# A hybrid transformer block on one core: the first local-attention query projection moved into the state-space core

## The chip, the cores and the metric

The kernel runs on one core of a Trainium2 chip, in one launch. The metric is the device time of that core in microseconds (us), as the median of the runs; lower is better. The engines are TensorE (PE), VectorE (DVE), ScalarE (ACT), GpSimd (POOL) and SyncE (SP, which issues most DMAs). Each engine works through its instructions in a fixed order; an instruction whose input isn't there makes those behind it on its engine wait as well.

## The reference

Two layers (DEPTH = 2) act on 256 latent tokens and, in layer 0, 256 context tokens, with a model width of 1024, all in float32. In each layer a normalized input is projected into three token mixers and three gates:

```python
(xbc_l, dt_l, k_l, v_l, ckv_l, kr_l, z_l, q_l, cq_l, gates_l) = split_cols(h_l @ w_in[i], IN_WIDTHS)
...
y_ssm_l, y_ssm_c = ssd_branch(...)      # Mamba-2 scan in both directions, 16 heads, gated by silu(z), RMS norm
y_swa_l, y_swa_c = swa_branch(...)      # local attention, 8 query heads of 128, 2 key/value heads
y_mla_l, y_mla_c = mla_branch(...)      # latent attention, 8 heads
x_l = x_l + gt1[:, None] * merge_branches(gates_l, y_ssm_l, y_swa_l, y_mla_l, ...)
x_l = x_l + gt2[:, None] * swiglu(modulate(x_l, norm2_g[i], sh2, sc2), w_ffn_in[i], w_ffn_out[i])
```

The change concerns the queries of the local attention. They are projected, normalized per head, and those of latent tokens rotated:

```python
ql = apply_axial_rope(rms_norm(q.reshape(bsz, n, 8, 128), q_g), *rope)
```

In layer 1 only the latent tokens are carried on.

## The kernel before, in words

**Precision.** Float32 products are made of three `fp32r` matmuls each: both operands are split into a high and a low part, and `mm3` (L146 to L148) adds hi*hi, hi*lo and lo*hi. A weight block of 128x1024 comes in by DMA (`raw`), ACT makes its high part (`hi`, L132) and DVE its low part (`lo`, L134). Token tiles have 128 rows: four in layer 0 (two latent, two context), two in layer 1.

**The order of the work.** The program is written as Python generators. `weave(main, fill)` (L57) runs a main generator and after each of its steps takes pieces of a fill generator, until the cost that these yield has used up the step's budget. `braid` (L71) and `chain` join fills, `drain` runs a rest to its end. What is written first has priority; a scheduler then puts each engine's instructions into an order by these priorities and by its own estimate of when the inputs will be there. The accumulators in PSUM come from three pools: `mm` (four buffers), `s` and `t` (two each); transposes and the core's `L930` share `t`.

**The stretch around the change** (`layer`, L1366):

- `ssm_core` (L823) is the main generator: (group, token tile, half) steps, 16 + 4 in layer 0 and 8 + 4 in layer 1, each with a budget F_SSM of 6.5 and 8.44. A step builds decay matrices on ACT, POOL and DVE (L889 `cb`, L910 `eb`, L911 `ef`), then PE multiplies them (`L922`, eight small matmuls, tile `s`) and adds the carried state (`L930`, tile `t`). `L932` scales the latter and `L934` adds the former (DVE, `yo`), `L940` (POOL) sums into `xs`, `L946` (DVE) multiplies by the gate `z`, and `L948` (ACT) sums its square.
- The fill is the gate projection `zproj`, then keys and values `swa_kv` braided with the first gates. Its yields add up to less than the core's budgets.
- Behind the core stands `ssm_out` (L977): the sums of squares (L982, L983), the reciprocal root on POOL (`ssr`, L160), the scaling of z (`L989`), and per 128 columns a transposition (`L995`) and the split into `yt` (L156, L157).
- Between the steps of `ssm_out` the code takes steps of `swa_q` (L1045), once per group g of four heads: q[0], then q[1]. A `swa_q` multiplies four weight blocks (96 matmuls of 128x512 in layer 0, 48 in layer 1, tiles `mm`), copies the result (ACT L1052 `qraw`), squares it (ACT L1054), sums per head (DVE `L1055`, `L1060`), takes the reciprocal root (POOL L160 `rsq`), multiplies it in (POOL `L1066`), rotates the latent tiles (`rope`: DVE `L555`, four `L561`, `L563`, tile `ro`), and transposes four heads (PE `L1076`, tile `t`), each followed by a split into high and low parts (`qT`).
- Then `attend` weaves the scores (mm3 into `s`, mask by `L1104`), the softmax (ACT L631) and the transposes of the probabilities (`L596`) with the remaining projections.

Of the kernel before, what the change touches and what calls it, by code (L numbers as in the profile page):

```python
# [70 lines left out]
def braid(n, a, b):  # L71

    for _ in range(n):
        yield next(a)
    for x in a:
        yield x
        y = next(b, None)
        if y is not None:
            yield y
    yield from b  # L80


def drain(gen):
    for _ in gen:
        pass


class Kern:
# [913 lines left out]
    def swa_kv(self, l, h):  # L1002
# [26 lines left out]
            w3 = lambda t: t[:, o].rearrange("p (h w) -> p h w", h=2)  # L1029
            self.rope(w3(ro), w3(kr[0]), p["rs"][1], tt, 2, P, w3(tmp))  # L1030
        yield 0.1
        self.kT, self.qT = [], {}
        for g in range(2):
            ps = self.PS("t")
            for tt in range(4):
# [256 lines left out]
    def gates(self, l, b, h, cols, out):  # L1292
        nc = self.nc
        n = cols.stop - cols.start
        for m in range(KT):
            ps = self.lin_a(self.d["w_g"][l, b * 8 + m], h, cols)
            if n == 512:
                t = self.U(name="gate")
                nc.scalar.activation(t, ps, AF.Tanh, scale=0.5)
                o = self.dr.tile([P, 512], F32, tag=f"gate{b}{m}", name=self.nm("gated"))  # L1300
                nc.scalar.dma_start(o, t)
                out.append(o)
            else:
                if m % 2 == 0:
                    u = self.U(name="gate")
                t = u[:, (m % 2) * 256 : (m % 2) * 256 + 256]
                nc.scalar.activation(t, ps, AF.Tanh, scale=0.5)
                out.append(t)
            yield n / 100
# [56 lines left out]
    def layer(self, l, x, h, norm):  # L1366
# [4 lines left out]
        tts = range(2) if last else range(4)  # L1371
        streams = (0,) if last else (0, 1)
        gt, merged = [[], [], []], [None] * KT
        gates = lambda b: self.gates(l, b, h, cols, gt[b])
# [2 lines left out]
        post = chain(self.ssm_inproj(l, h, norm), () if l else self.tables(l))  # L1377
        for _ in range(5):
            next(post)
        fill = chain(self.zproj(l, h, tts), braid(4, self.swa_kv(l, h), gates(0)))  # L1380
        drain(self.ssm_conv(l, h, last, post, fill))
        drain(post)
        if l == 0:
# [2 lines left out]
        drain(fill)  # L1386
        rows = iter(()) if last else self.mod_rows()
        next(rows, None)
        q = [self.swa_q(l, h, g, tts) for g in range(2)]

        out = self.ssm_out(tts)
        for _ in range(NQ):
            next(out, None)
            next(q[0])
        for _ in range(5):
            next(out, None)
            next(q[0], None)
            next(q[1])
        drain(out)
        drain(q[0])  # L1400
        ys = self.yssm
        self.pair, self.cqT = {}, None
        mod = iter(())
# [82 lines left out]
        h = []  # L1486
# [191 lines left out]
```

## Time and profile before

| | |
|---|---|
| median of 3 runs | 1853.46 us (1852.89 to 1855.38) |
| profiled execution: its own time | 1853.35 us |
| profiled execution: span of the core | 1851.5 us |
| mean granted TensorE clock | 0.999 |
| PE, DVE, ACT, POOL busy | 97%, 76%, 49%, 16% |
| chain that ended last | PE 67%, DVE 9%, issue 4%, ACT 4%, POOL 2% |

The time is that of the whole launch, the span runs from the first to the last instruction in the trace. Busy shares are means over the span. A row of a timeline gives an instruction's start, its duration, engine, source line, operation and tiles; a bracket at its end gives how long its engine had been idle before it and whose work ended that. Durations of consecutive matmuls overlap, so a matmul's price is read from start to start.

### The profile page before, as it was taken

Reading aid. Unit: us, or ns where it says so; the run is one execution under the profiler, and the core shown is the slowest. Engines: PE = TensorE matmul, PEld = TensorE weight load, DVE = VectorE, ACT = ScalarE, POOL = GpSimd, SP = SyncE. Lnnn points to the kernel's source line nnn. Section 1 sums busy time; section 2 is a strip of 40 time slices with the busy share of each in tenths; the row PEclk is TensorE's granted clock in tenths of the full one; section 3 lists DMA queues with packets and bytes.
Section 4 is the critical chain, followed back from the end, with each engine's and each line's share of the span. In section 5 each row is a group of like instructions: output and inputs, shape, how many; then the busy total and the mean of one; then the engine's idle time right before and its main releaser. Section 6 shows DMA issues by size and latency. Waiting matters only on the chain.

```text
span 1851.5 us, 28424 instructions
## 1 busy us (share of the span) xinstructions
PE 1797.0 (97%) x10180; PEld 1534.7 (83%) x10180; DVE 1411.7 (76%) x3090; ACT 916.3 (49%) x2025; POOL 294.0 (16%) x265
## 2 busy tenths in 40 slices
PE   8999999999999999999999999999999999999999
PEld 2886777778888888898888888887779988899999
DVE  3896876897799885569888875798788688786654
ACT  2557674444545653333323222547745677455442
POOL 3005433200013331100000000002421022210000
PEclk9999999999999999999999999999999999999999
DMA  8234353454443233536556553335334332255565
GB/s 301 91 106 149 113 176 99 136 199 158 136 166 105 99 120 113 189 109 198 193 184 203 183 188 117 105 103 182 117 123 135 107 106 85 90 181 171 183 181 139
DMA packets 102750, 270.22 MB, mean 146 GB/s; under 512 B 12897, under 2 KB 15761, under 8 KB 102609
## 3 DMA queue, kind: packets, MB, share of 16 engines
q1 hardware_dynamic: 93888, 254.06, 42.3%
q10 hardware_dynamic: 7056, 9.85, 1.5%
q0 software_dynamic: 1664, 4.50, 0.6%
q8 instruction: 80, 1.31, 0.3%
q14 instruction: 62, 0.50, 0.1%
HBM read 256.70 MB, written 11.67 MB: 145 GB/s over the span
## 4 chain that ended last, share of the span: by engine, by line
PE 67%; DVE 9%; issue 4%; ACT 4%; POOL 2%; DMA 1%; SPq 0%; POOLq 0%; ACTq 0%; DVEq 0%
PE mm L146 20%; PE mm L147 20%; PE mm L148 20%; DVE lo L134 3%; ACT hi L132 2%; PE t L596 1%; DVE junk L253 1%; PE s L146 1%; PE s L148 1%; PE s L147 1%; DMA eb<-scr 1%; DVE ptl L154 1%; DMA mraw<-in_w_modT 1%; DVE rmax L623 0%; POOL ef L896 0%
## 5 line engine op out<-in xcount | busy, mean ns | idle before, releaser
L132 ACT ACTIVATE hi<-raw 128x1024 fp32r<-128x1024 f32 (+1 forms) x350 | 356.7, 1021 | 582.1 <-PE mm L147 290.2
L134 DVE TENSOR_TENSOR lo<-raw,hi 128x1024 fp32r<-128x1024 f32 (+3 forms) x346 | 425.2, 1231 | 195.6 <-ACT hi L132 194.0
L146 PE MATMUL mm<-hh,hi 128*128 128x512 f32 (+1 forms) x1280 | 438.5, 345 | 4.1 <-ACT sq L676 1.9
L148 PE MATMUL mm<-hh,lo 128*128 128x512 f32 (+1 forms) x1280 | 435.8, 341 | 0.9 <-DVE lo L134 0.9
L147 PE MATMUL mm<-hl,hi 128*128 128x512 f32 (+1 forms) x1280 | 436.0, 341 | 0.6 <-DVE hl L346 0.5
L146 PEld LDWEIGHTS mm<-hh,hi 128*128 128x128 f32 x1280 | 241.7, 190 | 32.4 <-ACT sq L676 2.2
L148 PEld LDWEIGHTS mm<-hh,lo 128*128 128x128 f32 x1280 | 242.5, 190 | 28.7 <-DVE lo L134 1.3
L147 PEld LDWEIGHTS mm<-hl,hi 128*128 128x128 f32 x1280 | 242.5, 190 | 28.0 <-DVE hl L346 1.2
L146 PE MATMUL mm<-hi,hh 128*128 128x512 f32 (+2 forms) x368 | 142.5, 387 | 3.3 <-ACT hh L312 2.0
L147 PE MATMUL mm<-lo,hh 128*128 128x512 f32 (+2 forms) x368 | 138.9, 378 | 0.0
L148 PE MATMUL mm<-hi,hl 128*128 128x512 f32 (+2 forms) x368 | 136.9, 381 | 2.0 <-DVE hl L346 2.0
L253 DVE CUSTOM_DVE_ANT_0 junk<-mraw,crow,mod 128x512 bf16<-128x512 f32 x160 | 120.3, 752 | 3.5 <-DMA mraw<-in_w_modT 1.2
L253 DVE CUSTOM_DVE_ANT_0 junk<-mraw,crow 128x512 bf16<-128x512 f32 x160 | 110.3, 690 | 13.1 <-DMA mraw<-in_w_modT 11.8
L631 ACT ACTIVATE prob<-s,nm 128x512 f32<-128x512 f32 (+1 forms) x96 | 59.1, 615 | 56.3 <-DVE nm L628 30.4
L153 ACT ACTIVATE pth<-t 128x256 fp32r<-128x256 f32 x160 | 60.5, 388 | 46.9 <-DVE ptl L154 38.6
L146 PEld LDWEIGHTS mm<-hi,hh 128*128 128x128 f32 x368 | 69.8, 190 | 16.7 <-ACT hh L312 2.5
L148 PEld LDWEIGHTS mm<-hi,hl 128*128 128x128 f32 x368 | 69.1, 190 | 14.4 <-DVE hl L346 2.5
L147 PEld LDWEIGHTS mm<-lo,hh 128*128 128x128 f32 x368 | 69.6, 189 | 11.9 <-issue 2.9
L160 POOL TENSOR_TENSOR nrs<-nv,mhalf 128x2 f32<-128x2 f32 x7 | 5.2, 743 | 436.8 <-DVE nv L294 436.8
L146 PE MATMUL mm<-acth,hi 128*128 128x512 f32 (+1 forms) x198 | 72.7, 367 | 0.6 <-DVE xl L1352 0.6
L148 PE MATMUL mm<-acth,lo 128*128 128x512 f32 (+1 forms) x198 | 72.3, 365 | 0.0
L147 PE MATMUL mm<-actl,hi 128*128 128x512 f32 (+1 forms) x198 | 72.3, 365 | 0.0
(429 smaller groups left out, 4063.1 us busy)
## 6 DMA issues: line engine op xcount, KB each, us to landing
raw<-in_w_fi SPq DMA_DIRECT2D x88, 512.0 KB, 3.4
mraw<-in_w_modT SPq DMA_DIRECT2D x160, 256.0 KB, 4.6
raw<-in_w_g SPq DMA_DIRECT2D x48, 512.0 KB, 3.4
raw<-in_w_p SPq DMA_DIRECT2D x48, 512.0 KB, 3.3
raw<-in_w_fo SPq DMA_DIRECT2D x32, 512.0 KB, 3.6
raw<-in_w_xbc SPq DMA_DIRECT2D x24, 512.0 KB, 3.6
wm<-in_w_mod SPq DMA_DIRECT2D x32, 256.0 KB, 5.6
raw<-in_w_z SPq DMA_DIRECT2D x16, 512.0 KB, 3.2
```

The source lines that it names most:

```text
L132: nc.scalar.activation(hi[:, :n], raw[:, :n], AF.Copy)
L134: eng.tensor_tensor(lo[:, :n], raw[:, :n], hi[:, :n].bitcast(F32), ALU.subtract)
L146: mm(out, a[0], b[0], start=start, stop=False)
L147: mm(out, a[0], b[1], start=False, stop=False)
L148: mm(out, a[1], b[0], start=False, stop=stop)
L153: nc.scalar.activation(hi, src, AF.Copy)
L154: nc.vector.tensor_tensor(lo, src, hi.bitcast(F32), ALU.subtract)
L160: self.nc.gpsimd.tensor_tensor(out, v, self.mhalf[:, 0 : v.free_size()], ALU.pow)
L253: nc.vector.tensor_tensor_reduce(junk, raw[j], self.crow[2 * s + j], 0.5, o if j else 0.0, ALU.mult, ALU.add, o)
L596: nc.tensor.transpose(tp[:, i * P : (i + 1) * P], pt[:, i * P : (i + 1) * P], self.ident)
L631: nc.scalar.activation(pt[:, :nk], ps[:, :nk], AF.Exp, bias=nm, scale=scale, accum_out=den)
```

## The change

Both query projections are created ahead of the core. q[0], all of it (projection, norm, rotation, transposes), is appended to the core's fill; q[1] goes between the steps of `ssm_out`, where q[0] went, and its rest, as before, beside the start of the attention. The dictionary of transposed queries is therefore made in `layer` and no longer in `swa_kv`.

```diff
@@ -1029,7 +1029,7 @@
             w3 = lambda t: t[:, o].rearrange("p (h w) -> p h w", h=2)
             self.rope(w3(ro), w3(kr[0]), p["rs"][1], tt, 2, P, w3(tmp))
         yield 0.1
-        self.kT, self.qT = [], {}
+        self.kT = []
         for g in range(2):
             ps = self.PS("t")
             for tt in range(4):
@@ -1377,7 +1377,9 @@
         post = chain(self.ssm_inproj(l, h, norm), () if l else self.tables(l))
         for _ in range(5):
             next(post)
-        fill = chain(self.zproj(l, h, tts), braid(4, self.swa_kv(l, h), gates(0)))
+        q = [self.swa_q(l, h, g, tts) for g in range(2)]
+        self.qT = {}
+        fill = chain(self.zproj(l, h, tts), braid(4, self.swa_kv(l, h), gates(0)), q[0])
         drain(self.ssm_conv(l, h, last, post, fill))
         drain(post)
         if l == 0:
@@ -1386,18 +1388,13 @@
         drain(fill)
         rows = iter(()) if last else self.mod_rows()
         next(rows, None)
-        q = [self.swa_q(l, h, g, tts) for g in range(2)]
 
         out = self.ssm_out(tts)
         for _ in range(NQ):
             next(out, None)
-            next(q[0])
-        for _ in range(5):
-            next(out, None)
-            next(q[0], None)
             next(q[1])
-        drain(out)
-        drain(q[0])
+        for _ in out:
+            next(q[1], None)
         ys = self.yssm
         self.pair, self.cqT = {}, None
         mod = iter(())
```

The matrix multiplications, and the instructions of DVE, POOL and SP, are the same in number and shape. Their order differs from the core's last steps on, in layer 0 until some way into the attention and in layer 1 likewise. Three places follow. Numbers behind names only tell tiles apart.

**PE, layer 0, the core's last step and q[0].** Before: the last matmuls of q[0] (`mm_536` to `mm_538`), then transposes of z (`t_558`) and the first transposes of q[0] (`t_561`).

```order
L148 MATMUL mm_538_2803<-hi_556_2902,hl_87_339 128x512
L146 MATMUL mm_538_2803<-hi_556_2902,hh_90_348 128x512
L147 MATMUL mm_538_2803<-lo_557_2903,hh_90_348 128x512
L148 MATMUL mm_538_2803<-hi_556_2902,hl_91_349 128x512
L995 MATMUL t_558_2930<-c_ident_79,z_292_1421 128x128
L995 MATMUL t_558_2930<-c_ident_79,z_293_1424 128x128
L995 MATMUL t_558_2930<-c_ident_79,z_294_1427 128x128
L995 MATMUL t_558_2930<-c_ident_79,z_295_1430 128x128
L1076 MATMUL t_561_2941<-c_ident_79,ro_545_2844 128x128
```

Now: the last matmuls of q[0] (`mm_495`), then the core's last `L922` and `L930`, then q[1] (`mm_548` and on).

```order
L146 MATMUL mm_495_2564<-hi_510_2701,hh_98_368 128x512
L147 MATMUL mm_495_2564<-lo_511_2702,hh_98_368 128x512
L148 MATMUL mm_495_2564<-hi_510_2701,hl_99_369 128x512
L922 MATMUL s_508_2687<-xs_260_1270,ef_476_2455 128x64 x4
L930 MATMUL t_512_2734<-hst_324_1564,cv_160_719 128x512
L146 MATMUL mm_548_2847<-hi_553_2853,hh_70_299 128x512
L147 MATMUL mm_548_2847<-lo_554_2854,hh_70_299 128x512
L148 MATMUL mm_548_2847<-hi_553_2853,hl_71_300 128x512
```

Thirty more rows on stands the first transpose of q[0] (`t_529`):

```order
L148 MATMUL mm_548_2847<-hi_556_2885,hl_83_329 128x512
L146 MATMUL mm_549_2848<-hi_556_2885,hh_78_318 128x512
L147 MATMUL mm_549_2848<-lo_557_2886,hh_78_318 128x512
L1076 MATMUL t_529_2786<-c_ident_79,ro_525_2767 128x128
L1076 MATMUL t_532_2797<-c_ident_79,ro_525_2767 128x128
L148 MATMUL mm_549_2848<-hi_556_2885,hl_79_319 128x512
```

The core's last `L922` and `L930` have moved behind the projection of q[0], and q[0]'s first transposes ahead of all transposes of z; between `L930` and them stand 32 matmuls of q[1].

**DVE, layer 0, from the head sums of q[0] (`ssq`) to its rotated tiles (`ro`).** Before, the core's end lies far ahead of these rows:

```order
L1060 TENSOR_SCALAR ssq_522_2767<-ssq_522_2767 128x16
L134 TENSOR_TENSOR lo_566_2955<-raw_564_2952,hi_565_2954 128x1024
L157 SCALAR_TENSOR_TENSOR ytl_544_2840<-t_542_2834,p_ssm_ng_104_383,yth_543_2839 128x512
L555 TENSOR_TENSOR ro_545_2844<-qraw_523_2768,rs_215_1034 128x512
L561 TENSOR_TENSOR rt_546_2845<-qraw_523_2768,rs_215_1034 128x4x32 x4
L563 TENSOR_TENSOR ro_545_2844<-ro_545_2844,rt_546_2845 128x512
```

Now:

```order
L932 TENSOR_TENSOR yo_513_2736<-t_512_2734,du_114_402 128x512
L934 TENSOR_TENSOR yo_513_2736<-yo_513_2736,s_508_2687 128x512
L1055 TENSOR_REDUCE ssq_515_2742<-sq_517_2745 128x4
L946 TENSOR_TENSOR z_349_1711<-z_349_1711,xs_260_1270 128x512
L1055 TENSOR_REDUCE ssq_515_2742<-sq_519_2750 128x4
L1055 TENSOR_REDUCE ssq_515_2742<-sq_521_2755 128x4
L1055 TENSOR_REDUCE ssq_515_2742<-sq_523_2760 128x4
L1060 TENSOR_SCALAR ssq_515_2742<-ssq_515_2742 128x16
L555 TENSOR_TENSOR ro_525_2767<-qraw_516_2743,rs_215_1034 128x512
L561 TENSOR_TENSOR rt_526_2768<-qraw_516_2743,rs_215_1034 128x4x32 x4
L555 TENSOR_TENSOR ro_527_2776<-qraw_518_2748,rs_215_1034 128x512
L563 TENSOR_TENSOR ro_525_2767<-ro_525_2767,rt_526_2768 128x512
```

The last `L932`, `L934` and `L946` of the core stand among the head sums of q[0], and the second rotation begins between `L561` and `L563` of the first.

**PE, layer 1, the first scaled z (`L995`).** Before, the last matmuls of q[0] (`mm_3042`) and some of q[1] (`mm_3067`) stand ahead of it:

```order
L146 MATMUL mm_3042_13573<-hi_3055_13640,hh_2735_11834 128x512
L147 MATMUL mm_3042_13573<-lo_3056_13641,hh_2735_11834 128x512
L148 MATMUL mm_3042_13573<-hi_3055_13640,hl_2736_11835 128x512
L146 MATMUL mm_3067_13682<-hi_3070_13686,hh_2704_11738 128x512
L147 MATMUL mm_3067_13682<-lo_3071_13687,hh_2704_11738 128x512
L148 MATMUL mm_3067_13682<-hi_3070_13686,hl_2705_11739 128x512
L995 MATMUL t_3052_13632<-c_ident_79,z_2887_12704 128x128
L995 MATMUL t_3057_13656<-c_ident_79,z_2887_12704 128x128
L146 MATMUL mm_3067_13682<-hi_3070_13686,hh_2707_11743 128x512
L147 MATMUL mm_3067_13682<-lo_3071_13687,hh_2707_11743 128x512
```

Now, behind q[0]'s transposes (not shown): scores of the local attention (`s_3120`, `s_3136`), and between them the core's last two `L930`.

```order
L148 MATMUL s_3120_13879<-kTh_2985_13234,qT_3057_13641 128x512
L1104 LDWEIGHTS identb_1272
L1104 MATMUL s_3120_13879<-maskb_1274,identb_1272 128x128
L930 MATMUL t_3065_13680<-hst_2998_13292,cv_2776_12129 128x512
L930 MATMUL t_3067_13684<-hst_2968_13115,cv_2776_12129 128x512
L146 MATMUL s_3136_13963<-kTh_2985_13234,qT_3057_13641 128x512
L147 MATMUL s_3136_13963<-kTl_2986_13235,qT_3057_13641 128x512
L148 MATMUL s_3136_13963<-kTh_2985_13234,qT_3057_13641 128x512
L1104 LDWEIGHTS identb_1272
L1104 MATMUL s_3136_13963<-maskb_1274,identb_1272 128x128
L995 MATMUL t_3084_13762<-c_ident_79,z_2887_12704 128x128
```

The two `L930` have moved from the middle of q[0]'s projection to behind its transposes, and between them and the first `L995` stands one block of scores instead of matmuls of q[0] and q[1].

## Rows read from the trace of the kernel before

**Rows 1.** Page, part 1: engine, busy us, share of the span, instructions.

```profile
PE 1797.0 (97%) x10180; PEld 1534.7 (83%) x10180; DVE 1411.7 (76%) x3090; ACT 916.3 (49%) x2025; POOL 294.0 (16%) x265
```

**Rows 2.** Timeline of PE, layer 0, end of the core (start us, us, instruction, [idle before <- releaser]).

```profile
281.32 1.00 PE L922 MATMUL s<-xs,ef 128*128 128x64 f32 x8
...
282.16 1.08 PE L930 MATMUL t<-hst,cv 128*128 128x512 f32 x2
...
284.78 1.12 PE L930 MATMUL t<-hst,cv 128*128 128x512 f32 x2 [0.63 <-DVE cb L889]
...
288.95 1.10 PE L922 MATMUL s<-xs,ef 128*128 128x64 f32 x8 [0.52 <-DVE ef L911]
...
293.15 0.39 PE L147 MATMUL mm<-lo,hh 128*128 128x512 f32 x1
...
309.02 0.39 PE L148 MATMUL mm<-hi,hl 128*128 128x512 f32 x1
```

**Rows 3.** Timelines of DVE, POOL and PE, layer 0, the query chains.

```profile
311.68 0.68 DVE L1055 TENSOR_REDUCE ssq<-sq 128x4 f32<-128x512 f32 x1
...
312.94 0.17 DVE L1060 TENSOR_SCALAR ssq<-ssq 128x16 f32<-128x16 f32 x1
...
313.18 2.90 POOL L160 TENSOR_TENSOR rsq<-ssq,mhalf 128x16 f32<-128x16 f32 x1 [14.88 <-DVE ssq L1060]
...
316.16 5.51 POOL L1066 TENSOR_TENSOR qraw<-qraw,rsq 128x512 f32<-128x512 f32 x4
...
318.86 0.87 DVE L555 TENSOR_TENSOR ro<-qraw,rs 128x512 f32<-128x512 f32 x1
...
319.65 2.58 DVE L561 TENSOR_TENSOR rt<-qraw,rs 128x128 f32<-128x128 f32 x4
...
322.26 0.69 DVE L563 TENSOR_TENSOR ro<-ro,rt 128x512 f32<-128x512 f32 x1
...
359.87 0.30 PE L1076 MATMUL t<-c_ident,ro 128*128 128x128 f32 x1 [1.44 <-DVE ro L563]
```

**Rows 4.** Busy time by stretch: us, PE, PEld, DVE, ACT, POOL busy, PEclk, DMA.

```profile
375.00:643.00 268.00, 262.89 (x1451) 225.86 (x1450) 230.96 (x672) 144.89 (x391) 47.79 (x51) 1.00 0.42 142
1344.30:1364.80 20.50, 18.78 (x85) 13.38 (x83) 16.62 (x22) 9.08 (x17) 9.41 (x7) 1.00 0.28 92
1364.80:1403.70 38.90, 35.16 (x234) 30.45 (x235) 35.32 (x70) 19.96 (x36) 9.16 (x6) 1.00 0.42 138
1403.70:1591.70 188.00, 183.84 (x1286) 168.37 (x1285) 151.47 (x408) 129.99 (x353) 35.68 (x31) 1.00 0.33 105
```

**Rows 5.** Timelines of DVE, POOL and PE, layer 1, core's end and query chains.

```profile
1356.76 0.68 DVE L934 TENSOR_TENSOR yo<-yo,s 128x512 f32<-128x512 f32 x1
...
1357.82 2.67 POOL L940 TENSOR_TENSOR xs<-xs,yo 128x512 f32<-128x512 f32 x2
...
1359.21 2.36 DVE L134 TENSOR_TENSOR lo<-raw,hi 128x1024 fp32r<-128x1024 f32 x1 [1.77 <-ACT hi L132]
...
1361.49 0.68 DVE L946 TENSOR_TENSOR z<-z,xs 128x512 f32<-128x512 f32 x1
...
1365.04 0.41 PE L995 MATMUL t<-c_ident,z 128*128 128x128 f32 x2 [0.89 <-DVE z L989]
...
1371.52 0.16 DVE L1060 TENSOR_SCALAR ssq<-ssq 128x8 f32<-128x8 f32 x1
...
1375.98 0.89 DVE L561 TENSOR_TENSOR rt<-qraw,rs 128x128 f32<-128x128 f32 x4
...
1378.00 0.30 PE L1076 MATMUL t<-c_ident,ro 128*128 128x128 f32 x1 [1.95 <-DVE ro L563]
...
1397.19 0.41 PE L1076 MATMUL t<-c_ident,ro 128*128 128x128 f32 x2 [1.56 <-DVE ro L563]
```

**Rows 6.** Busy time by stretch, early in the program (columns as in rows 4).

```profile
35.40:42.50 7.10, 5.48 (x29) 3.10 (x29) 3.93 (x10) 3.33 (x6) 4.72 (x4) 1.00 0.29 98
42.60:46.00 3.40, 3.40 (x12) 3.40 (x13) 3.40 (x10) 2.04 (x4) 0.00 (x0) 0.50 0.82 270
```

## The prediction, made before the changed kernel ran

> **What bounds the kernel now.** I read the profile from the page inwards: the busy share of the engines, then busy time by stretch, then single instructions and their waits. The page first: TensorE (PE) is busy 97% of the span [rows 1]. The matrix instructions are the same in both kernels, as many and of the same shapes; only their sequence changes. So the change cannot take work off PE. It can only remove or add *waits* of PE, and all that follows counts those. The reader should look at the number in brackets at the end of a PE row: the idle time before it and who ended it.
>
> How much waiting is there to win? In layer 0 the end of the state-space core shows two waits, 0.63 us before an `L930` and 0.52 before an `L922` [rows 2]: the fill has run out there and the core's own DVE chain is late. Further behind, a transpose of q[1] waits 1.44 for its rotated tile [rows 3]; q[0]'s wait for nothing. In layer 1 the stretch 1344.3 to 1403.7 holds 59.4 us, of which PE is busy 18.78 + 35.16 = 53.94, so 5.5 us idle [rows 4]; the named waits in it are 0.89 for the scaled z (`L995`) and 1.95 and 1.56 for rotated queries (`L1076`) [rows 5]. All of it together is about 8 us, 0.4% of the time. A measurement of this kernel tells some 0.2%, 3.7 us, from no change.
>
> **Prices.** 128x512 matmuls follow one another every 0.227 us: 70 of them between the rows at 293.15 and 309.02 [rows 2]. The `L922` of one step (a row of x8) hold PE 0.84 (281.32 to 282.16), an `L930` (a row of x2) at most its 1.08 [rows 2].
>
> **Layer 0, step by step.** The projection of q[0] fills the core's last steps. What goes: the 0.63 and 0.52, so -1.15. The last `L922` and `L930` of the core now come *behind* q[0]'s last matmul, which in before ended at 309.02 + 0.23 = 309.25; so that matmul ends at 309.25 - 1.15 - 0.84 - 1.08 = 306.2. What PE has from there until the first transpose of q[0], by the order shown above: `L922` 0.84, `L930` 1.08, 32 matmuls of q[1] at 0.227 = 7.26. So PE stands at that transpose at 315.4.
>
> When is its tile there? In before the way from the last matmul to the rotated tile took until 322.26 + 0.69 = 322.95, 13.7 us [rows 2, 3]. The change shortens it little, because DVE now has the core's end among the reductions: `L946` of the core's last step stands behind the first of the four `L1055`, and it waits for `L930`, `L932`, `L934` and the addition on POOL (`L940`). From the end of `L930` (308.1): `L932` and `L934` 0.68 each [rows 5], `L940` half of 2.67 = 1.33, `L946` 0.68: 311.5. Three `L1055` of 0.68 [rows 3] bring 313.5, less some 0.5 since DVE's rows overlap by 0.08 each: 313.0. `L1060` to the first `L1066` is 316.16 - 312.94 = 3.2 us [rows 3], nearly all of it the reciprocal root on POOL; so `L1066` starts at 316.2 and, at a quarter of 5.51, the first tile is there at 317.6. Then `L555` 0.87, four `L561`, `L555` again, `L563` 0.69.
>
> The four `L561` are the open price: they took 0.89 alone in layer 1 [rows 5], but 2.58 beside POOL's `L1066` [rows 3]. So the tile is ready between 320.6 and 322.3, and PE waits 5.2 to 6.9. I take 6.2, nearer the upper end, because the four `L1066` run from 316.2 to 321.7 here too, right beside the rotation. The Trainium skill, "SBUF — State Buffer", section "SBUF: two separate sides", says that DVE and GpSimd hold their shared port pair as an exclusive lock and the loser blocks fully; that would give the upper end, 6.9, and the two rows bear it out.
>
> The second rotated tile follows with 0.2 more of waiting. Behind it PE has 46 matmuls of q[1] (10.4 us) before it needs the scaled z, which covers that chain at no cost; without this cover it would cost what it costs in layer 1 (below). q[1]'s own chain now runs beside the output transposes, where q[0]'s did: there I put the waits equal, +-1. The 1.44 [rows 3] stays in that: the rotation is late in another place. **Layer 0: -1.15 + 6.2 + 0.2 = +5.2** (from 3.2 to 7).
>
> **Layer 1.** It has two token tiles, so half the matmuls to hide behind. Two waits go: what the core's end idles in 1344.3 to 1364.8, 20.50 - 18.78 = 1.7 less 0.8 that belongs to `L995`, so 0.9 [rows 4]. In before q[0]'s last matmul ended three matmuls and the 0.89 ahead of `L995`: 1365.04 - 0.89 - 0.7 = 1363.4 [rows 5]. Now the 0.9 goes, and two steps' `L922` (1.7) and two `L930` (2.2) come behind it: 1358.6. It is followed by those `L922` and 30 matmuls of q[1] (6.8): 8.5 us of cover, to 1367.1. The way to the rotated tile is at least 9.6 us, if `L1060` follows the last matmul by 3.7 as in layer 0 of before (309.25 to 312.94 [rows 2, 3]) and the rest takes 1371.52 to 1378.00, less 0.6 for foreign DVE work, 5.9 [rows 5]. It is at most 11.5, if `L946` delays the reductions as in layer 0. So PE waits 1.1 to 3.0; I take 2.6, near the upper end, since the order does put `L946` in front.
>
> Then comes the costliest step. The last two `L930` of the core now stand *behind* these transposes and the first attention scores (the order of PE in layer 1 shows it). On them hang `L932`, `L934`, `L940`, `L946`, the square, the root and `L989`, and at its end `L995`. In before, from the start of `L940` to `L995` that was 1365.04 - 1357.82 = 7.2 us [rows 5], hidden under 10.9 us of matmuls but for 0.89. Now one score block of 0.8 us stands between. Of the 7.2, about 1.3 were delays by a foreign `L134`, and 1.3 is the first of the two `L940`, which runs early; `L932` and `L934` add 1.2. That is 5.8 without and 7.1 with the foreign work, less 0.8: PE waits 5.0 to 6.3. I take 5.4, nearest to the chain without foreign work, since DVE has little else then. The second rotated tile and the first mask add 0.3 and 0.8. The 0.89 of before goes. In the stretch behind (`L1055`, rotation of q[1], output tiles, all on DVE) before waited 1.95 + 1.56 = 3.5 [rows 5]; with q[1] later and the scores already waiting I count 4.2, +0.7. **Layer 1: -0.9 - 0.9 + 2.6 + 0.3 + 0.8 + 5.4 + 0.7 = +8.0** (from 5 to 10).
>
> **Clock.** After a sparse stretch (PE busy 5.48 of 7.10 us) the granted clock fell to 0.50, the lower of its two levels (1.2 of 2.4 GHz), for the next 3.4 us [rows 6], and half of those, 1.7, were lost. The new waits make a sparser stretch in each layer. I count a part of 1.7 twice: **+2.2** (from 0, if it does not fall, to 5, if it stays low through layer 1).
>
> **What comes back.** The attention stretches behind idle 268.00 - 262.89 = 5.1 and 188.00 - 183.84 = 4.2 us [rows 4]. A PE that arrives later finds some of that ready: **-1** (from 0 to -5).
>
> DMA: w_q's weight blocks are loaded in another place of SP's queue, as many as before, and the tiles that they wait for come free earlier; I cost that at nothing, because PE's waits of before name no w_q load.
>
> **Sum**, against the profiled execution's 1853.35 (the span is 1851.5; the median of the runs, 1853.46, stands 0.1 above it): 5.2 + 8.0 + 2.2 - 1 = +14.4, so **1867.7 us**.
>
> **Rivals.**
>
> *Faster: the tiles are ready in time.* The mechanism is the first query chain hidden under q[1]'s matmuls. It decides at 9.2 us (layer 0) and 8.5 us (layer 1) from q[0]'s last matmul to its rotated tile, and at 0.8 us for z in layer 1. Then 0.63, 0.52, 1.44 and layer 1's 5.5 go: 1853.35 - 8.1 = 1845 us. For it: q[0] starts earlier, and the waits it covers are real [rows 2]. Against: the chain took 13.7 us in before. Chance 0.07.
>
> *Paid back.* The waits come, but the attention stretches give all their 9.3 us of idle back and the clock holds: 1853.35 + 13.2 - 9.3 = 1857 us. For it: DVE, which those stretches wait for, has its rotations behind it. Against: their waits are spread over many short ones. Chance 0.10.
>
> *The clock stays low.* From the first wait of layer 1 to about 1390 PE would have some 11 us of work in 23; at half clock that work takes 22, of which 5 do not fit beside the waits: 1867.7 + 5 = 1873 us. For it: the fall in [rows 6] came after far less idling. Against: it lasted 3.4 us only. The Trainium skill, "TensorE: Matmul & The Clock Gate", section "HAM oscillation — how this bites in real kernels", says that idle gaps take the clock to half and that repeated ones keep a kernel cold; it speaks against this change and would give this case. The trace agrees in its one fall after sparse work; no run here shows repeated ones. Chance 0.13.
>
> *It does not do what it says.* The scheduler already put q[0]'s matmuls among the core's last steps: in before, too, `lo,hh` and `hi,hl` matmuls with w_q stand ahead of its end [rows 2]. If the two orders wait alike, 1853.4. Against: `L930` has moved behind the projection. Chance 0.04.
>
> **How the numbers follow.** Forecast 0.66, faster 0.07, paid back 0.10, low clock 0.13, nothing 0.04. The forecast's terms span 1853.35 + (3.2 + 5 + 0 - 5) = 1856.6 to 1853.35 + (7 + 10 + 5 - 0) = 1875.4. The range 1856 to 1877 leaves out the faster case, no effect and half of "paid back". Slower by over 0.2% (above 1857.1): 0.66 + 0.13 + some 0.04 of paid back = 0.83. Within: 0.10. Faster: 0.07.
>
> **What would show it.** Right: `L1076 <- ro L563` with 5 to 7 us in layer 0 near 315 and about 2.6 near 1367; `L995 <- z L989` with about 5 in layer 1; the waits 0.63 and 0.52 gone; the granted clock at 0.50 behind a long wait. Wrong: PE at `L1076` in layer 0 with under 3 us of wait would fell the largest term, `L995` in layer 1 under 2 the second.

## The result, and the profile after

The changed kernel takes 1894.63 us (median of 4 runs, 1894.49 to 1895.38) against 1854.42 for the kernel before beside it: a ratio of 1.0217, 95% interval 1.0205 to 1.0229. It is slower, as forecast, but by 40 us where 14 were forecast, and outside the range. The profiled execution took 1894.61, its span 1892.8, that is 41.3 more than before.

The page of the changed kernel, PE's line of part 1 and the granted clock in 40 slices of part 2:

```profile
PE 1813.6 (96%) x10180; PEld 1546.1 (82%) x10180; DVE 1415.6 (75%) x3090; ACT 918.2 (49%) x2025; POOL 286.2 (15%) x265
...
PEclk9999998999999999999999999999989999999999
```

PE was busy 1797.0 us before [rows 1], with the same matmuls. So of the 41.3 us, 1813.6 - 1797.0 = **16.6 are matmuls that took longer**, and the rest, 24.7, is PE standing idle (both as the page reckons a matmul's end). The 8 in the clock's line at slices 7 and 30 show where: the two stretches of the change. The same line of the kernel before has a 9 in all 40 slices.

To see what each stretch lost, both traces are cut where PE's matmuls have moved equally many columns (a 128x512 matmul moves 512), which is equal work; the numbers of instructions (x) differ a little, because their order does. Busy time by stretch (columns as in rows 4), first of before, then of after: the core's end with q[0], the output beside q[1], the last third of layer 0's attention, layer 1's core end and output.

```profile
280.20:334.70 54.50, 53.35 (x261) 43.65 (x260) 36.43 (x60) 22.34 (x40) 15.02 (x11) 1.00 0.31 102
334.70:375.20 40.50, 36.62 (x178) 28.55 (x177) 38.04 (x87) 20.60 (x44) 10.08 (x8) 1.00 0.47 163
538.30:645.50 107.20, 103.44 (x591) 88.98 (x590) 95.18 (x268) 63.28 (x188) 31.91 (x33) 1.00 0.34 114
1344.30:1403.80 59.50, 54.04 (x320) 43.94 (x319) 52.04 (x91) 29.05 (x53) 18.57 (x13) 1.00 0.37 123
```

```profile
279.50:343.70 64.20, 55.47 (x258) 44.90 (x257) 38.49 (x66) 25.36 (x49) 14.00 (x11) 0.92 0.26 86
343.70:388.30 44.60, 40.40 (x190) 31.07 (x190) 35.37 (x75) 19.37 (x38) 9.15 (x8) 0.92 0.33 118
552.10:668.40 116.30, 107.13 (x593) 91.07 (x592) 100.11 (x285) 66.99 (x201) 32.12 (x37) 0.97 0.31 106
1367.20:1442.80 75.60, 61.45 (x324) 51.47 (x323) 52.82 (x102) 31.60 (x60) 15.28 (x13) 0.89 0.27 96
```

The spans go from 54.5 to 64.2, 40.5 to 44.6, 107.2 to 116.3 and 59.5 to 75.6. Three of the four are no surprise as places; the third was forecast to win. Idle time is the span less the first number after it (PE busy): 1.2 to 8.7, 3.9 to 4.2, 3.8 to 9.2, 5.5 to 14.2. In the second stretch PE idles hardly more, and still 4.1 us are lost: the granted clock, 1.00 before, is 0.92.

### The profile page after: what moved, and what is told of

Read it like the earlier page. It is cut to its first block, busy times and chain, and to the rows that moved or that the text cites. A ratio compares the mean times of both kernels' runs of the same rounds, so it can differ in the third digit from the quotient of the medians.

```text
span 1892.8 us, 28434 instructions
## 1 busy us (share of the span) xinstructions
PE 1813.6 (96%) x10180; PEld 1546.1 (82%) x10180; DVE 1415.6 (75%) x3090; ACT 918.2 (49%) x2025; POOL 286.2 (15%) x265
## 4 chain that ended last, share of the span: by engine, by line
PE 67%; DVE 8%; issue 5%; POOL 3%; ACT 2%; DMA 1%; SPq 0%; POOLq 0%; DVEq 0%; ACTq 0%
PE mm L146 20%; PE mm L147 20%; PE mm L148 20%; DVE lo L134 2%; PE t L596 1%; POOL rsq L160 1%; ACT hi L132 1%; DVE junk L253 1%; PE s L146 1%; PE s L148 1%; DMA mraw<-in_w_modT 1%; PE s L147 1%; DVE rt L561 0%; PE s L922 0%; DVE ptl L154 0%
## 5 line engine op out<-in xcount | busy, mean ns | idle before, releaser
L132 ACT ACTIVATE hi<-raw 128x1024 fp32r<-128x1024 f32 (+2 forms) x350 | 356.5, 1020 | 576.5 <-PE mm L147 282.6
L148 PEld LDWEIGHTS mm<-hi,hl 128*128 128x128 f32 x368 | 69.8, 192 | 14.4 <-DVE hl L346 2.5
L762 DVE SCALAR_TENSOR_TENSOR cv<-cx,p_convw,cv 128x508 f32<-128x508 f32 (+3 forms) x96 | 70.8, 738 | 1.7 <-ACT cv L753 0.2
```

What stands on the lines that cost most here:

```text
L132: nc.scalar.activation(hi[:, :n], raw[:, :n], AF.Copy)
L148: mm(out, a[1], b[0], start=False, stop=stop)
L762: nc.vector.scalar_tensor_tensor(r3(v)[:, :, o], r3(x)[:, :, i], w[:, m, j : j + 1], r3(v)[:, :, o], ALU.mult, ALU.add)
```

## The experiments

Each is timed against the kernel before on the same chip as itself. The table sums up their profiled executions: us by which a stretch is longer than in the one profiled execution of before, cut at equal columns of PE's matmuls. The stretches are (start) all that lies ahead; (A) core's end, layer 0; (B) output; (C) attention's first part; (D) its last third; (E) from there to the core's end of layer 1; (F) core's end and output, layer 1; (G) its attention. What lies behind G differs by 0.4 at most. Where an edit moves other work across a cut (gates and q[0]: start and A, E and F), the two are to be added.

| run | median us | ratio (95%) | start | A | B | C | D | E | F | G |
|---|---|---|---|---|---|---|---|---|---|---|
| the change | 1894.6 | 1.0217 (1.0205-1.0229) | -0.7 | 9.7 | 4.1 | 0.7 | 9.2 | -0.1 | 16.2 | 1.9 |
| e1, layer 0 | 1879.1 | 1.0129 (1.0114-1.0144) | -0.4 | 9.7 | 4.4 | 0.0 | 9.7 | 0.6 | 0.0 | 1.5 |
| e2, layer 1 | 1871.9 | 1.0088 (1.0071-1.0104) | 0.6 | 0.0 | 0.0 | 0.3 | -0.3 | 0.4 | 15.8 | 3.1 |
| e3, q[1] as before | 1877.9 | 1.0124 (1.0109-1.0140) | -2.0 | 10.5 | 1.0 | 0.4 | -0.3 | 0.2 | 13.8 | -0.2 |
| e4, projection only | 1881.9 | 1.0145 (1.0130-1.0160) | -0.5 | 18.6 | -0.5 | 0.1 | 0.5 | 0.1 | 8.8 | 1.1 |
| e5, gates behind q[0] | 1880.9 | 1.0146 (1.0124-1.0169) | 1.5 | 0.3 | 4.0 | 0.0 | 10.0 | 4.6 | 3.6 | 1.9 |
| e6, e5 and e3 | 1863.6 | 1.0051 (1.0036-1.0066) | -0.3 | 2.4 | 0.9 | 0.1 | 0.6 | 4.5 | 2.0 | -0.7 |
| e7, q[1] alone | 1880.2 | 1.0136 (1.0119-1.0153) | -0.1 | 0.0 | 2.4 | 2.1 | 11.7 | 0.4 | 6.9 | 3.6 |
| e8, tail behind core | 1892.5 | 1.0201 (1.0184-1.0219) | -1.7 | 11.1 | 3.2 | 0.0 | 9.4 | 0.0 | 9.4 | 3.1 |
| e10, scaling on DVE | 1884.7 | 1.0162 (1.0149-1.0175) | 1.7 | 6.7 | 0.4 | -0.4 | 9.2 | 0.2 | 10.5 | 3.5 |
| e11, before, scaling on DVE | 1861.0 | 1.0028 (1.0016-1.0040) | -0.2 | 0.0 | 1.1 | 0.5 | 1.9 | 0.4 | 0.2 | 3.8 |
| e12, e6, scaling on DVE | 1866.9 | 1.0062 (1.0050-1.0074) | 5.5 | 6.4 | -1.3 | 0.5 | -0.1 | -0.5 | 3.5 | -0.3 |
| e13, layer 1, tail behind core | 1866.8 | 1.0065 (1.0051-1.0079) | 0.1 | 0.0 | 0.1 | 0.3 | 1.0 | 1.2 | 10.5 | 3.1 |

The start holds up to some 2 us either way that no edit brings: within the first 67 us the granted clock is at 0.50 for 3.4 us once in the execution of before, never in those of e3 and e6, and twice in those of e10 and e12; PE's 850th instruction starts at 213.0, 210.8 or 210.9, and 214.7 or 215.0.

**e1 and e2: each layer alone.** The edit of `layer` is made for l == 0 or l == 1 only, with the lines of before for the other.

```diff
-        fill = chain(self.zproj(l, h, tts), braid(4, self.swa_kv(l, h), gates(0)), q[0])
+        fill = chain(self.zproj(l, h, tts), braid(4, self.swa_kv(l, h), gates(0)), q[0] if l == 0 else ())
```

> The change in layer 0 alone; layer 1 as in the kernel before. Theory A (each layer loses for itself): layer 0 of the changed kernel is 23.5 us longer than before from the core's end to the end of the attention, layer 1 17.6; so 1854 + 23.5 = 1878 us here. Rival B (the loss of layer 1 is a consequence of what layer 0 left late): then layer 1 would still lose here, 1885 us or more.

> The change in layer 1 alone. Theory A: 1854 + 17.6 = 1872 us. Rival B: layer 1 loses less than 8 us when layer 0 is as before, under 1862 us.

1879.1 and 1871.9: each layer loses for itself, 25 and 18 us; together that is 43 where both at once lose 40. The stretches of the table repeat those of the whole change to 0.7 us (G in layer 1 to 1.2). Rival B falls. So the two layers can be read apart.

**e3 and e7: each query group alone.** e3 keeps q[0] in the fill and gives q[1] its place of before:

```diff
         for _ in range(NQ):
             next(out, None)
-            next(q[1])
-        for _ in out:
-            next(q[1], None)
+        for _ in range(5):
+            next(out, None)
+            next(q[1])
+        drain(out)
```

> q[0] in the core's fill as in the change, but q[1] takes its five steps where it took them before, and its rest lies beside the attention again. Theory A: the late attention of layer 0 (107.2 us before, 115 now) lost because q[1]'s rest is no longer among its fills, and DVE's split of the output waits behind q[1]'s rotation; both go, about 8 + 5 us back, so 1880 to 1884 us, with the wait of 7.8 us for q[0]'s rotated tile still there. Rival C (all of it follows from q[0]'s rotation and transposes in the fill): stays at 1892 to 1896 us.

e7 leaves q[0] where it was and takes all of q[1] ahead of the attention:

```diff
-        for _ in range(5):
-            next(out, None)
-            next(q[0], None)
-            next(q[1])
-        drain(out)
+        for _ in out:
+            next(q[0], None)
+            next(q[1], None)
         drain(q[0])
+        drain(q[1])
```

> The other half of the change alone: q[0] beside the output as before, but all of q[1] ahead of the attention instead of only its first five steps. Theory A (q[1]'s rest, 4 units of some 1 us, is missing among the attention's fills in the last heads of layer 0): the late attention of layer 0 is 7 to 9 us longer than before, core's end as before: 1860 to 1866 us. Rival C (what fails there is brought by q[0]'s place): 1852 to 1857 us.

e3 came out at 1877.9, better than Theory A had it: stretch D falls from +9.2 to -0.3, B gains 3 us, F and G 2 each. e7 came out at 1880.2, worse than either theory had it, and there D is +11.7, without any change at the core of layer 0. In all runs D is long (9.2 to 11.7) where layer 0's q[1] is done ahead of the attention, and at most 1.9 where it is not. PE's long waits in the last part of layer 0's attention, in the changed kernel:

```profile
555.99 0.63 PE L1245 MATMUL t<-c_ident,qraw 128*128 128x128 f32 x4 [2.17 <-DVE nm L628]
...
590.56 0.63 PE L596 MATMUL t<-c_ident,prob 128*128 128x128 f32 x4 [0.93 <-DVE nm L626]
...
594.16 0.50 PE L146 MATMUL s<-kTh,qTh 128*128 128x512 f32 x1 [1.22 <-ACT prob L631]
...
598.21 1.09 PE L596 MATMUL t<-c_ident,prob 128*128 128x128 f32 x4 [2.62 <-DVE nm L626]
...
602.42 0.50 PE L147 MATMUL mm<-ysl,hi 128*128 128x512 f32 x1 [1.42 <-DVE ysl L154]
```

In e3, where q[1]'s rest is beside the attention again, two short ones are left:

```profile
586.62 0.63 PE L596 MATMUL t<-c_ident,prob 128*128 128x128 f32 x4 [1.49 <-DVE nm L626]
...
590.14 0.50 PE L147 MATMUL mm<-ysl,hi 128*128 128x512 f32 x1 [0.43 <-DVE ysl L154]
```

and in e7 the same transposes and scores wait as in the changed kernel, to 0.03 us (two of them):

```profile
584.91 0.51 PE L146 MATMUL s<-kTh,qTh 128*128 128x512 f32 x1 [1.21 <-ACT prob L631]
...
588.97 1.09 PE L596 MATMUL t<-c_ident,prob 128*128 128x128 f32 x4 [2.65 <-DVE nm L626]
```

At the rows from 590 on PE waits on the softmax (`nm`, `prob`, the tiles of the step just issued) and on what follows from it (`ysl`): from 590 to 599 its order holds the attention's own matmuls and four transposes (`kraw`), nothing else. Attention in this kernel is fed by `other`, a chain of fills that each head draws from by a fixed budget. In the kernel before, the last seven pieces of q[1] (3.7 units, by the code's own count) stand at its front. With q[1] finished beforehand, every head draws what it drew, and the last gate is handed out one step of the attention earlier. What is next in the chain (`branch1`, the projection of the local attention's result, the `ysl` rows) yields only empty pieces until the last local head is done; by the code's yields and budgets there are 35 of these, over five steps, where before has 23 over four.

The wait of 2.17 is of another kind: matmuls of a gate stand behind those transposes in PE's order, and DVE, which releases them, is busy for 4.93 us from 550 to 555. e7 has it too (2.15 at 546.57), e3 does not. That a longer chain at that place would cure D was not tried otherwise than by e3.

The section on the change says that q[1]'s rest lies beside the start of the attention "as before". It does not. `ssm_out` has 13 steps in layer 0 and 11 in layer 1, the changed code takes a piece of q[1] with each of them, and q[1] has 12 pieces; before, five were taken there. So of the seven that lay beside the attention none is left in layer 0 and one in layer 1.

**e5 and e6: the same fill in another order.** q[0]'s projection covers the chain of keys and values, and the gates stand behind q[0]; e6 has e3's edit as well.

```diff
-        fill = chain(self.zproj(l, h, tts), braid(4, self.swa_kv(l, h), gates(0)), q[0])
+        fill = chain(self.zproj(l, h, tts), braid(4, self.swa_kv(l, h), braid(4, q[0], gates(0))))
```

> The same fill in another order: q[0]'s projection beside the keys' and values' chain, its norm, rotation and transposes beside the first gates, whose matmuls then stand behind q[0]. Theory A (q[0]'s chain lacked matmuls to hide under): the wait for q[0]'s rotated tile falls from 7.8 us to under 1, the scaled z of layer 1 waits under 2 instead of 4.9, no long fall of the clock at the core's end; what is left is q[1] beside the output, 8 to 13 us: 1862 to 1868 us. Rival D (the chain loses because DVE and POOL are held by the core itself, wherever its cover stands): the waits only move into the core, 1880 us or more.

> Both cures together: the gates behind q[0] in the fill, and q[1] as before. If the two losses are separate and add, the stretches give +1.0 at layer 0's core, +3.5 at its output, -1 in its attention and +5 to +8 in layer 1: 1861 to 1867 us. Rival F (each cure only moves the wait to the other place): 1872 us or more.

e5 is a miss in its sum (1880.9, a time that Rival D allows) and a hit at its place: start and A together fall from +9.0 to +1.8, and E with F from 16.1 to 8.2, so the waits did not move into the core, as Rival D has it. The wait for the first rotated tile fell to 2.18, not to under 1. What I had put at 8 to 13 us for q[1] is 4.0 + 10.0 in layer 0 alone. e6, at 1863.6, is inside its expectation: the two cures add, and 30 of the 40 us are gone. The waits for the first rotated tiles in e6, layer 0 and layer 1:

```profile
283.47 0.33 PE L1076 MATMUL t<-c_ident,ro 128*128 128x128 f32 x1 [2.13 <-DVE ro L563]
...
1352.62 0.45 PE L1076 MATMUL t<-c_ident,ro 128*128 128x128 f32 x1 [4.46 <-DVE ro L563]
```

In layer 0 the 7.75 us have become 2.13, in layer 1 3.79 have become 4.46. A gate of layer 1 has 256 columns, half the matmul time of layer 0's; that this is why its chain stays uncovered was not tried. e6 is still 0.5% slower than before. No version here beats the kernel before.

**e4: only the projection in the fill.** The steps between those of `ssm_out` are the lines of before, so q[1] has its place of before, as in e3.

```diff
-        fill = chain(self.zproj(l, h, tts), braid(4, self.swa_kv(l, h), gates(0)), q[0])
+        fill = chain(self.zproj(l, h, tts), braid(4, self.swa_kv(l, h), gates(0)), islice(q[0], 4))
```

> Only q[0]'s projection goes into the core's fill; its norm, rotation and transposes run beside the output steps as before, and q[1] takes its five steps as before. Theory A (q[0]'s chain behind the core has too few matmuls beside it, wherever its later part is written): PE still waits 7 to 10 us in layer 0 for the rotated tile or the scaled z, 2 to 4 in layer 1, and the late attention is as before: 1866 to 1874 us. Rival E (the place of the rotation and transposes is all that costs): 1850 to 1858 us.

1881.9, worse than either theory and than e3 (1877.9), in which all of q[0] is in the fill: A is +18.6. Beside the wait for the rotated tile there is a second. ACT, then PE, of e4:

```profile
312.11 0.63 ACT L948 ACTIVATE sq<-z 128x512 f32<-128x512 f32 x1 [4.82 <-DVE z L946]
...
316.08 0.65 ACT L1054 ACTIVATE sq<-mm 128x512 f32<-128x512 f32 x1
...
313.85 0.80 PE L146 MATMUL mm<-hi,hh 128*128 128x512 f32 x1 [6.52 <-ACT sq L1054]
...
329.68 0.45 PE L1076 MATMUL t<-c_ident,ro 128*128 128x128 f32 x1 [8.38 <-DVE ro L563]
```

The copies and squares of q[0]'s accumulators (`L1052`, `L1054`) are now written behind the core's last step, so on ACT they stand behind the square of z (`sq<-z`), which idles 4.82 us until DVE delivers z. All four `mm` accumulators stay occupied meanwhile, and q[1]'s projection, whose matmuls need one, waits 6.52. Taking only the matmuls ahead leaves what empties them behind.

**e8 and e13: the rank of the core's last step.** q[0]'s rotation and transposes are written behind the core's last step, in both layers (e8), or with layer 0 as before (e13).

```diff
+        fill = chain(self.zproj(l, h, tts), braid(4, self.swa_kv(l, h), gates(0)), islice(q[0], 6))
...
         drain(fill)
+        drain(q[0])
```

> As the changed kernel, but q[0]'s rotation and transposes are written behind the core's last step instead of in its fill, so they no longer rank ahead of the core's last two state matmuls of layer 1. Theory P (these two matmuls stood behind the transposes for their rank, and the scaled z of layer 1 waited on them): the wait of 4.9 us for z and those of 1.5 and 0.6 ahead of it in layer 1 fall to 2 or less together, with part of the fallen clock behind; layer 0 as in the changed kernel: 1884 to 1889 us. Rival G (z waits because DVE is busy with the queries, rank or not): 1892 to 1896 us.

> The change in layer 1 alone (1871.9 us without this edit), with q[0]'s rotation and transposes written behind the core's last step. With layer 0 as before, less else varies than in the run of both layers, where the traces differed by 7 us in this stretch but the times overlapped. Theory P (rank of the core's last state matmuls): 1863 to 1867 us. Rival G (their rank does not matter for the time): 1870 us or more.

PE's waits in layer 1 of the changed kernel, and below two rows of e13:

```profile
1393.38 0.66 PE L1076 MATMUL t<-c_ident,ro 128*128 128x128 f32 x2 [3.79 <-DVE ro L563]
...
1402.48 1.98 PE L930 MATMUL t<-hst,cv 128*128 128x512 f32 x4 [1.54 <-DVE qT L154]
...
1405.11 0.50 PE L146 MATMUL s<-kTh,qT 128*128 128x512 f32 x1 [0.65 <-DVE yo L934]
...
1411.10 1.39 PE L995 MATMUL t<-c_ident,z 128*128 128x128 f32 x4 [4.95 <-DVE z L989]
```

```profile
1378.09 0.66 PE L1076 MATMUL t<-c_ident,ro 128*128 128x128 f32 x2 [2.88 <-DVE ro L563]
...
1387.41 0.91 PE L995 MATMUL t<-c_ident,z 128*128 128x128 f32 x4
```

In e13 the transposes of z have no bracket: PE waits for nothing there. The waits of 1.54, 0.65 and 4.95 are gone, the one for the rotated tile is 2.88; new ones of 1.65 and 0.99 have come, and one for the split output has grown from 1.45 in e2 to 2.84. Stretch F falls from 15.8 in e2 to 10.5; by time e13 stands at 1866.8, a ratio of 1.0065 (1.0051 to 1.0079) against e2's 1.0088 (1.0071 to 1.0104): within what Theory P expects, with intervals that overlap a little. By time e8 speaks for neither: 1892.5 lies where Rival G has it, and its interval overlaps that of the change. Its trace shows the same as e13's, F down from 16.2 to 9.4, but is of its fastest execution (1888.1). So the waits' cause is shown by the traces, and their price, weakly, by e13 alone.

**e10, e11 and e12: a shorter chain.** The multiplication `L1066` moves from POOL to DVE, in the changed kernel (e10), in the kernel before (e11) and in e6 (e12).

```diff
-            nc.gpsimd.tensor_tensor(v4(qr[tt]), v4(qr[tt]), rs[:, tt, :].unsqueeze(2).to_broadcast([P, 4, P]), ALU.mult)
+            nc.vector.tensor_tensor(v4(qr[tt]), v4(qr[tt]), rs[:, tt, :].unsqueeze(2).to_broadcast([P, 4, P]), ALU.mult)
```

> The changed kernel with the four multiplications of the queries by their reciprocal root on DVE instead of POOL, so that POOL no longer works beside the rotation. Theory A (the wait is the chain less its cover, and the rotation is stretched by POOL's work: four products 2.57 us beside it, 0.89 alone): the wait of 7.8 us for q[0]'s rotated tile falls to 4 to 5.5, that of 3.8 us for the split output by 1 to 2, layer 1's 3.8 by 1 or more; with the clock's share 1882 to 1889 us. Rival H (POOL is not what stretches it, and DVE with more work is later still): 1893 us or more.

> The same edit in the kernel before. Theory A: its waits of 1.4 to 2 us for rotated tiles (three named ones, 4.9 us) each lose 1 us or more: 1849 to 1852 us. Rival H: DVE, busy 37.8 of 40.7 us beside layer 0's output, gets 0.7 us per tile more: 1854 to 1858 us.

> The same edit on top of both cures (gates behind q[0], q[1] as before). Theory A: the waits for rotated tiles there (2.1, 2.9 in layer 0, 4.5, 1.7 in layer 1) fall by 4 us or more together: 1856 to 1860 us. Rival H: 1863 us or more.

e10: 1884.7, as Theory A has it. The four products of the rotation on DVE, and PE's wait:

```profile
321.08 0.89 DVE L561 TENSOR_TENSOR rt<-qraw,rs 128x128 f32<-128x128 f32 x4
...
324.46 0.66 PE L1076 MATMUL t<-c_ident,ro 128*128 128x128 f32 x2 [4.65 <-DVE ro L563]
```

0.89 instead of 2.57 us, and 4.65 instead of 7.75. In the output the wait of 3.80 for the split (`ytl`, below) fell to 0.93. In the two others Theory A fell: e11 took 1861.0 (ratio 1.0028, 1.0016 to 1.0040; slower, and by more than Rival H has it), e12 1866.9 (1.0062, 1.0050 to 1.0074; no better than e6). Beside layer 0's output DVE is busy 38.04 of 40.50 us in before (second row of its windows above), so there what POOL no longer does is likely to delay DVE's other work. In e11's trace the three waits for rotated tiles (1.44, 1.95, 1.56) are 1.93, 1.25 and none, but one of 1.20 at the matmuls of the split output has come in layer 1, and one of 1.75 before scores early in its attention. In e12's the first rotated tile of layer 0 waits 3.86 instead of 2.13, that of layer 1 3.35 instead of 4.46. In these runs a shorter chain paid where PE waited on it long, and not where DVE was full.

## Why the prediction was wrong

The direction and most places were right, the size was not. Two steps failed: the attention, which was to give 1 us back and lost 8, and the clock, put at 2.2 and measured at 16.6. The four terms, with the idle times (span less PE busy) of the stretches:

| term | forecast | measured |
|---|---|---|
| waits, layer 0's core and output (A, B) | +5.2 | +7.9 |
| waits, layer 1's core and output (F) | +8.0 | +8.7 |
| waits in the attention, "what comes back" (C, D, G) | -1 | +8.4 |
| clock (PE's busy time) | +2.2 | +16.6 |
| sum | +14.4 | +41.6, the span +41.3 |

By the steps of the prediction:

**Layer 0, first transpose: right, a little small.** The working said that PE stands at the transpose at 315.4, the tile is ready between 320.6 and 322.3, and PE waits 6.2. PE's timeline of the changed kernel:

```profile
305.13 1.00 PE L922 MATMUL s<-xs,ef 128*128 128x64 f32 x8
...
305.96 1.08 PE L930 MATMUL t<-hst,cv 128*128 128x512 f32 x2
...
308.02 0.50 PE L146 MATMUL mm<-hi,hh 128*128 128x512 f32 x1 [0.98 <-ACT sq L1054]
...
315.18 0.39 PE L147 MATMUL mm<-lo,hh 128*128 128x512 f32 x1
...
323.32 0.66 PE L1076 MATMUL t<-c_ident,ro 128*128 128x128 f32 x2 [7.75 <-DVE ro L563]
...
324.20 0.63 PE L146 MATMUL mm<-hi,hh 128*128 128x512 f32 x1
...
324.63 0.63 PE L147 MATMUL mm<-lo,hh 128*128 128x512 f32 x1
...
329.58 0.39 PE L146 MATMUL mm<-hi,hh 128*128 128x512 f32 x1
...
329.80 0.39 PE L147 MATMUL mm<-lo,hh 128*128 128x512 f32 x1
```

The core's last `L922` and `L930` come first, then 32 matmuls of q[1], of which the last starts at 315.18; then the wait, 7.75. The chain, from DVE and POOL:

```profile
311.13 0.69 DVE L946 TENSOR_TENSOR z<-z,xs 128x512 f32<-128x512 f32 x1 [0.88 <-POOL xs L940]
...
313.64 0.17 DVE L1060 TENSOR_SCALAR ssq<-ssq 128x16 f32<-128x16 f32 x1
...
313.90 2.91 POOL L160 TENSOR_TENSOR rsq<-ssq,mhalf 128x16 f32<-128x16 f32 x1 [2.80 <-DVE ssq L1060]
...
317.96 1.51 DVE L555 TENSOR_TENSOR ro<-qraw,rs 128x512 f32<-128x512 f32 x1 [4.14 <-POOL qraw L1066]
...
319.39 2.57 DVE L561 TENSOR_TENSOR rt<-qraw,rs 128x128 f32<-128x128 f32 x4
...
322.49 0.68 DVE L563 TENSOR_TENSOR ro<-ro,rt 128x512 f32<-128x512 f32 x1
```

`L946` does stand among the reductions, `L1060` starts at 313.64 (reckoned: 313.0), the root takes 2.91, the four `L561` the long value, 2.57. Short by 0.9 us were `L555`, which is stretched as well (1.51, reckoned 0.87), and the gaps between engines. Not in the sum at all was 0.98 before q[1]'s first matmul: its accumulator waits for ACT's square of q[0], as in e4. That PE still stood at the transpose at 315.6, as reckoned, is luck: the core's last `L922` came 1.1 us earlier than the working has it (305.13, not 306.2). The four `L561` one by one:

```profile
L561 DVE TENSOR_TENSOR rt<-qraw,rs x4: 279/700/1124, 319.4 to 321.7; 128x128 f32<-128x128 f32 x4
```

That is the shortest, the median and the longest in ns: two took 1.12 us, those that ran beside POOL's multiplications, and two 0.28, the ones behind the last of these. The rule of the Trainium skill ("SBUF — State Buffer", section "SBUF: two separate sides": an exclusive lock on a port pair, between a DVE instruction with two inputs from SBUF and a GpSimd instruction that reads SBUF, for the whole of the instruction that has it) pointed at the upper end; the trace agrees, by these two values, and so does e10, without POOL's multiplications: 0.89 for all four.

**"q[1]'s own chain ... there I put the waits equal": the sum held, their shape did not.** PE's idle time beside the output is 3.9 us before and 4.2 now. But it is one wait, not three, and the clock fell behind it. Beside the output, DVE has q[1]'s rotation in front of work that PE needs sooner. DVE, then PE, of the changed kernel:

```profile
349.07 1.51 DVE L555 TENSOR_TENSOR ro<-qraw,rs 128x512 f32<-128x512 f32 x1 [1.81 <-POOL qraw L1066]
...
350.50 2.58 DVE L561 TENSOR_TENSOR rt<-qraw,rs 128x128 f32<-128x128 f32 x4
...
353.00 0.74 DVE L157 SCALAR_TENSOR_TENSOR ytl<-t,p_ssm_ng,yth 128x512 fp32r<-128x512 f32 x1
...
353.79 0.79 PE L147 MATMUL mm<-ytl,hi 128*128 128x512 f32 x1 [3.80 <-DVE ytl L157]
```

A split of the output (`ytl`) had to wait behind `L555` and `L561` of q[1], and these for POOL. PE idles 3.80 us for it: about as much as the three waits of before together (0.65, 1.44 and 1.79), but in one piece. PE's busy time in the stretch rose from 36.62 to 40.40 us for the same work, which is nearly all that it lost.

What all of q[1]'s move costs is not one number. The change is 17 us slower than e3, which differs from it in q[1]'s place alone; e7 loses 25 to before, but there both queries' chains run beside the output, which they do not in the change, so that e3's 23 and e7's 25 add up to more than the 40.

**"What comes back", -1: this step failed, it has the wrong sign.** The attention idled 8.4 us more, 5.4 of them in the last third of layer 0's, where q[1]'s rest was missing among the fills (e3, e7); with the clock that third lost 9.2. The prediction took that rest to be where it was, asked only what a later PE would find ready, and did not ask what the moved steps had been hiding there.

**Layer 1: right mechanism, mis-sized.** z waits 4.95 (reckoned 5.4) and e13 shows that the rank of the last two `L930` is its cause; the rotated tile waits 3.79 (2.6), and 1.54 ahead of `L930` was not in the sum: that matmul shares the `t` accumulators with the transposes and waits until DVE has split one (`qT`). Idle time in F grew by 14.2 - 5.5 = 8.7 us, where 8.0 was reckoned; the other 7.4 of its 16.2 us are the clock.

**Clock, +2.2: this step failed, it is an eighth of what was lost.** Matmuls took 16.6 us more in all. In layer 0, behind the first wait:

```profile
315.40:323.30 7.90, 0.17 (x1) 0.01 (x1) 5.34 (x8) 0.00 (x0) 5.94 (x5) 0.67 0.00 0
323.30:329.00 5.70, 5.68 (x19) 4.64 (x20) 2.50 (x6) 0.25 (x1) 0.00 (x0) 0.55 0.28 92
329.00:335.00 6.00, 6.00 (x32) 4.89 (x31) 4.68 (x12) 4.47 (x11) 1.01 (x1) 1.00 0.18 59
```

The clock falls within the idle stretch and is at 0.55 on the mean of the next 5.7 us; matmuls follow one another every 0.43 us (324.20, 324.63) instead of 0.22 (329.58, 329.80). I had counted one fall per layer. From the core's end of layer 0 on there are seven stretches at the lower level, from 318, 352, 557 and 598 us in layer 0 and from 1393, 1410 and 1424 in layer 1, and none in before. Their spans and PE's busy time in them, in all:

```profile
sum 40.80, PE 32.06 PEld 26.35 DVE 26.72 ACT 9.11 POOL 7.62; mean PE 4.58 PEld 3.76 DVE 3.82 ACT 1.30 POOL 1.09
```

Half of 32.06 is 16.0, which accounts for the 16.6. The Trainium skill, "TensorE: Matmul & The Clock Gate", section "HAM oscillation — how this bites in real kernels", says that idle gaps bring the clock down again and again; the trace agrees, and its case, a rival with 0.13, was nearer to the truth in its mechanism than the forecast. It was not one long stay at the low level, though. That keeping PE busy through a wait would have kept the clock was not tried.

**The rivals.** "The tiles are ready in time" fell with 7.75 and 3.79 us of wait. "Paid back" fell with D and G. "It does not do what it says" fell: q[0]'s projection does fill the core's end, and the 0.63 and 0.52 of before [rows 2] are gone. That was all it could win.

Measured by stretch, -0.7 + 9.7 + 4.1 + 0.7 + 9.2 - 0.1 + 16.2 + 1.9 and 0.4 behind G make 41.4, against the span's 41.3 (the cuts lie between instructions).

## What to carry to other kernels

Work that is moved to fill a gap has a place that it leaves: ask what it hid there, and whether a fill with a fixed budget now runs dry at its far end. A fill should end in work without a tail of its own: with the gates behind q[0] instead of in front of it, the same instructions lost some 7 us less up to the end of layer 0's core. And where PE is the bound, price a new long wait with the clock: here one wait of 3.80 us was followed by a fall to 0.50 and three of before that sum to 3.9 were not.

## What the runs showed of the hardware

Beside POOL's multiplications, DVE's four 128x128 products took 2.57 us in place of 0.89, and a 128x512 product 1.51 in place of 0.69 (e10 has both values without POOL). POOL's reciprocal root grows with its columns: 0.71 us for 2, 1.65 for 8, 2.91 for 16.

Behind the waits of 3.79, 3.80 and 7.75 matmuls started every 0.43 us, and the waits of before, up to 1.95, left the clock at 1.00 [rows 4, 5]. No bound on a wait follows from that. The same place of layer 0's attention in before and in e11, just behind a wait of 1.57 in the one (to 577.08) and of 1.66 in the other (to 579.21):

```profile
578.70:582.10 3.40, 2.98 (x15) 2.27 (x14) 3.40 (x7) 2.50 (x6) 3.33 (x4) 1.00 0.84 292
580.80:584.20 3.40, 3.40 (x10) 2.63 (x10) 3.40 (x6) 2.50 (x6) 3.36 (x4) 0.50 0.78 286
```

The clock stayed at 1.00 in the one and was at 0.50 in the other; what decides it, these runs do not show.
